# Padding SBUF pools so that matmul operands share an offset modulo 512, with a rewritten routing stage, in a hybrid diffusion block with 16 experts

## The chip, the cores and the metric

The kernel runs on one core of a Trainium2 chip. The metric is the device time of one execution in microseconds. Three runs of the kernel before gave 2228.50, 2229.75 and 2232.72 us.

## What is computed

One layer over 1024 tokens of width 1024, with 256 context tokens ahead of it: a conditioned RMSNorm, an input projection, a Hyena long convolution beside a gated linear recurrence, an output projection with a gated residual, then a mixture of 16 SwiGLU experts in which each expert picks its 128 best tokens, and a last RMSNorm. The change touches the output projection's second half, the routing and the experts. Of the reference, that is:

```python
x = x + g1 * mix                                # mix: concatenated mixer outputs @ w_out[l]
h2 = modulate(rmsnorm(x, norm2_g[l]), sh2, sc2)  # h * (1 + scale) + shift
x = x + g2 * ec_moe(h2, router_w[l], exp_w1[l], exp_w3[l], exp_w2[l])

def ec_moe(h, router_w, w1, w3, w2):
    aff = jax.nn.softmax(jnp.einsum('bnd,de->bne', h, router_w).astype(jnp.float32), axis=-1)
    gates, idx = lax.top_k(jnp.swapaxes(aff, 1, 2), cap)
    xg = jax.vmap(lambda hb, ib: hb[ib])(h, idx)
    a = jnp.einsum('becd,edf->becf', xg, w1)
    b = jnp.einsum('becd,edf->becf', xg, w3)
    y = jnp.einsum('becf,efd->becd', jax.nn.silu(a) * b, w2)
    y = y * gates[..., None].astype(y.dtype)
    return jax.vmap(lambda yb, ib: jnp.zeros((N, D), yb.dtype).at[ib.reshape(-1)].add(yb.reshape(-1, D)))(y, idx)
```

Here cap is 128, D is 1024 and the experts' inner width is 2048. All inputs are float32.

## The kernel before

**Split products.** A float32 product is made of three matmuls of type fp32r. Each operand is split into a high part and what is left of it, and `mm3` (lines 63 to 66) issues high by high (L64), high by low (L65) and low by high (L66) into one accumulating PSUM tile. The first operand of `mm3` is the stationary one, 128x128; the second moves, 128x512 in all the calls that matter here. In the profile's names, `pa<-ehi,hcT` is a matmul with the moving operand `ehi` and the stationary operand `hcT`.

**Output projection, second half.** For token tiles t = 0 to 7, `finish_h` (L999) projects the Hyena half of the mixer output and adds it into the residual tile `oxt`. The moving operand is `wo`. The stationary operand is `hcT` (the same buffers under the name mxA) for t = 0 to 3, and `mx` for t = 4 to 7. Beside it the tile runs through `normed` (a Square over 1024 columns on ACT, eleven small DVE operations for the inverse root in `rsqrt`, and a multiplication into `oh`), `flip` (eight PE transposes and eight scaled ACT copies of 128 columns, L1026), `route` (eight matmuls with the router's weights), `affinity` (softmax) and `rows8`, which transposes the result into the row tile R (L1054). The loop at L1056 runs 11 times, and a tile's routing lags its projection by three rounds.

**Search.** When R is complete, ten rounds on DVE (L1096 to L1113) find each expert's threshold: a count over R (L1097), a comparison, a small update of `base` (L1106), one PE matmul (L1108), and the new threshold (L1109). Meanwhile ACT casts the first three weight pieces to their high parts, and POOL subtracts to get their low parts (L1189). After the search the positions are counted on PE (L1129 to L1134), DVE builds a one-hot tile (L1150), PE makes indices from it (L1154), and POOL gathers the first expert's 128 rows (L1159).

**Experts.** The weights come as 384 pieces of 1 MiB, 24 to an expert, through a ring of 13 `raw` buffers filled by SP's queue (`fetch`, L993). Piece by piece ACT casts raw to `ehi` (L1185) and DVE subtracts to get `elo` (L1191), in a ring of three (NHI = 3). PE takes a piece by 12 matmuls of `mm3`, so an expert is 288 split matmuls and all sixteen are 4608. Two thirds have `hcT`, the gathered rows transposed, as stationary operand; one third has `hh`, the gated inner activations. `take` (L1213) lets the piece two ahead be split when PE's code for the present piece is written; there is no planner behind it. After each expert, POOL adds its rows into the output in DRAM (L1274).

**Addresses.** The tiles lie in SBUF pools one behind the other, so an added tile moves all that follows in its pool and in the pools behind. In the built program the offsets within a partition modulo 512 bytes are: hcT 96, mx 0, wo 0, ehi and elo 448, hh 288. Both operands of the input projection (hT, whi) are at 0.

## Time and profile before

| | us |
|---|---|
| median of three runs | 2229.75 |
| the profiled execution | 2229.96 |
| its span, first to last instruction | 2228.2 |
| output projection, second half (PE) | 931 to 984 |
| rest of the routing, search, first gather | 984 to 1046.5 |
| experts, first to last split matmul | 1046.5 to 2201.7 |
| sums and last norm | 2201.7 to 2228.2 |

The profiled execution spent 1.8 us outside its span. Times in the trace count from the first instruction. PE, DVE, ACT and POOL each run their own queue in order; a row of the timeline is a group of like instructions on one engine, and what stands in square brackets is the idle time before it and what ended that. Matmuls overlap, so a matmul's duration is longer than the distance between two starts; the distance is what counts.

### The profile page before, as it was taken

How to read it: one execution, taken by the hardware profiler on the slowest of the kernel's cores; microseconds unless marked ns; L12 is line 12 of the kernel's file. 1: busy time of each engine (PE TensorE's matmuls, PEld its weight loads, DVE VectorE, ACT ScalarE, POOL GpSimd, SP SyncE). 2: the span in 40 equal slices, each digit the busy share in tenths (PEclk: the TensorE clock that was granted, in tenths of full speed). 3: DMA queues.
4: the chain of work that ended last, by engine and by line, in shares of the span. 5: the costliest groups of instructions: out<-in, count | busy, mean ns of one | idle time of the engine just before them, and what ended most of it. 6: DMA issues, size and time to landing. Idle time of an engine off the chain costs nothing.

```text
span 2228.2 us, 30347 instructions
## 1 busy us (share of the span) xinstructions
PE 2073.0 (93%) x11727; PEld 1621.2 (73%) x11727; DVE 1741.0 (78%) x2033; ACT 1256.0 (56%) x1492; POOL 198.3 (9%) x234
## 2 busy tenths in 40 slices
PE   7996999899999998983999999999999999999997
PEld 2443877788788876762888887777777777777775
DVE  6688366647878886557888888888888888988887
ACT  3566235334432211261777777677777777777775
POOL 1121100100000001123000000000000000000000
PEclk9999999899999999995999999999999999999999
DMA  7875412221152447474999999999999999999992
GB/s 250 269 261 162 142 44 81 82 77 43 49 161 81 128 139 262 127 261 177 365 373 365 369 381 354 362 353 365 363 360 359 355 369 364 356 354 374 356 361 101
DMA packets 248124, 565.94 MB, mean 254 GB/s; under 512 B 15545, under 2 KB 26380, under 8 KB 247981
## 3 DMA queue, kind: packets, MB, share of 16 engines
q1 hardware_dynamic: 209620, 477.88, 59.9%
q0 software_dynamic: 28784, 76.46, 11.3%
q10 hardware_dynamic: 9576, 9.67, 1.3%
q8 instruction: 92, 1.51, 0.3%
q14 instruction: 52, 0.42, 0.1%
HBM read 522.59 MB, written 41.50 MB: 253 GB/s over the span
## 4 chain that ended last, share of the span: by engine, by line
PE 75%; DVE 10%; issue 6%; DMA 5%; ACT 4%; POOL 1%; DVEq 0%; ACTq 0%; SPq 0%; POOLq 0%
PE pa L65 15%; PE pa L66 14%; PE pa L64 14%; PE pb L65 5%; PE pb L66 5%; PE pb L64 5%; DVE elo L1191 2%; PE pt L861 2%; PE pb L842 2%; PE pf L543 2%; PE pt L1278 1%; ACT sa L1175 1%; DVE arena L724 1%; DVE arena L722 1%; DMA oraw<-in_w_out 1%
## 5 line engine op out<-in xcount | busy, mean ns | idle before, releaser
L1191 DVE TENSOR_TENSOR elo<-raw,ehi 128x2048 fp32r<-128x2048 f32 x381 | 863.8, 2288 | 107.8 <-ACT ehi L1185 106.6
L1185 ACT CAST ehi<-raw 128x2048 fp32r<-128x2048 f32 x384 | 732.9, 1914 | 175.1 <-PE pa L66 133.4
L65 PE MATMUL pa<-elo,hcT 128*128 128x512 f32 x1024 | 408.6, 399 | 17.0 <-DVE elo L1191 16.9
L64 PE MATMUL pa<-ehi,hcT 128*128 128x512 f32 x1024 | 409.5, 401 | 1.4 <-ACT hcT L1176 1.4
L66 PE MATMUL pa<-ehi,hcT 128*128 128x512 f32 x1024 | 404.2, 395 | 0.0
L65 PEld LDWEIGHTS pa<-elo,hcT 128*128 128x128 f32 x1024 | 192.8, 188 | 73.9 <-DVE elo L1191 32.3
L64 PEld LDWEIGHTS pa<-ehi,hcT 128*128 128x128 f32 x1024 | 192.7, 188 | 45.5 <-ACT hcT L1176 1.8
L66 PEld LDWEIGHTS pa<-ehi,hcT 128*128 128x128 f32 x1024 | 192.6, 188 | 45.4
L65 PE MATMUL pb<-elo,hh 128*128 128x512 f32 x512 | 205.9, 402 | 0.3 <-DVE elo L1191 0.3
L66 PE MATMUL pb<-ehi,hh 128*128 128x512 f32 x512 | 203.1, 397 | 0.0
L64 PE MATMUL pb<-ehi,hh 128*128 128x512 f32 x512 | 191.2, 396 | 0.7 <-ACT hh L1281 0.7
L64 PE MATMUL pa<-hT,whi 128*128 128x512 f32 x448 | 178.0, 397 | 0.0
L66 PE MATMUL pa<-hT,wlo 128*128 128x512 f32 x448 | 177.7, 397 | 0.3 <-DVE wlo L577 0.3
L65 PE MATMUL pa<-hT,whi 128*128 128x512 f32 x448 | 175.9, 393 | 0.0
L1274 POOL DMA_INDIRECT xacc<-xg,idx x15 | 45.4, 3023 | 813.7 <-DVE xg L1269 813.7
L64 PEld LDWEIGHTS pb<-ehi,hh 128*128 128x128 f32 x512 | 96.4, 188 | 24.3 <-ACT hh L1281 0.9
L65 PEld LDWEIGHTS pb<-elo,hh 128*128 128x128 f32 x512 | 96.5, 188 | 22.3 <-DVE elo L1191 0.7
L66 PEld LDWEIGHTS pb<-ehi,hh 128*128 128x128 f32 x512 | 96.5, 188 | 22.1 <-issue 0.5
L66 PEld LDWEIGHTS pa<-hT,wlo 128*128 128x128 f32 x448 | 84.1, 188 | 18.7 <-DVE wlo L577 1.3
L65 PEld LDWEIGHTS pa<-hT,whi 128*128 128x128 f32 x448 | 84.2, 188 | 17.0 <-issue 0.2
L64 PEld LDWEIGHTS pa<-hT,whi 128*128 128x128 f32 x448 | 84.2, 188 | 16.8 <-issue 0.2
L543 PE MATMUL pf<-Yh,mt 128*128 128x256 f32 x256 | 74.3, 424 | 17.9 <-ACT he L549 6.5
(398 smaller groups left out, 3136.6 us busy)
## 6 DMA issues: line engine op xcount, KB each, us to landing
raw<-in_exp_w SPq DMA_DIRECT2D x371, 1024.0 KB, 8.3
aw<-in_ada_w SPq DMA_DIRECT2D x96, 256.0 KB, 4.8
wraw<-in_w_in SPq DMA_DIRECT2D x64, 256.0 KB, 3.2
raw<-in_exp_w POOLq DMA_DIRECT2D x13, 1024.0 KB, 9.4
mt<-in_fwm POOLq DMA_DIRECT2D x64, 128.0 KB, 3.7
Hd<-he ACTq DMA_DIRECT2D x32, 256.0 KB, 2.9
wod<-arena POOLq DMA_DIRECT2D x32, 256.0 KB, 3.4
arena<-in_fwm SPq DMA_DIRECT2D x32, 256.0 KB, 6.1
```

The costliest lines, as they stand in the source:

```text
L64: PE.matmul(ps, lhs[0], rhs[0], start=first, stop=False)
L65: PE.matmul(ps, lhs[0], rhs[1], start=False, stop=False)
L66: PE.matmul(ps, lhs[1], rhs[0], start=False, stop=last)
L543: PE.matmul(pt[:, :HC], mt[:, i, :], Y[:, 2 * n + i, :], start=(i == 0), stop=(i == 1))
L722: V.tensor_tensor(kv, kv, view(F2, h, [[2 * h, nb], [LT - h, 2], [0, h]]), ALU.mult)
L724: V.tensor_tensor(qv, qv, view(F2, LT + h, [[2 * h, nq], [-(LT + h), 2], [0, h]]), ALU.mult)
L842: PE.matmul(px[:, j, :], fm[:, j, i, :], Y[:, 2 * n + i, :], start=(i == 0), stop=(i == 1))
L861: PE.matmul(pz[:, j, :], im[:, i, j, :], pp[:, i, :], start=(i == 0), stop=(i == 1))
L1175: S.activation(hf[:, c, :], pt[:, c * P:(c + 1) * P], AF.Identity, scale=gs2[:, k:k + 1], bias=mod2[:, k, 0:1])
L1185: S.copy(hi, raw)
L1191: V.tensor_tensor(lo, raw, f32(hi[:]), ALU.subtract)
L1274: G.indirect_dma_start(xacc[:], bass.IndirectOffsetOnAxis(ap=idx[:, 0:1], axis=0), xg[:, 0:D], None, compute_op=ALU.add)
```

## The change

Four things are done.

- Three unused tiles are allocated: 40 floats in the pool `late`, 112 in `op`, 40 in `ep`. After it every operand of the output projection's and the experts' split products is at 96 modulo 512. Five of the thirteen `raw` buffers (pool `eb`) and all `ehi` and `elo` move by 160 bytes; the other eight `raw` buffers stay.
- The routing stage works on the rows of `oxt` before their normalisation: the router's weights are scaled once (`router`), PE transposes `oxt`, two ACT copies of 512 columns take the place of the eight scaled ones, and the inverse root is applied to the 16 logits. The Square is made in two halves, the inverse root has one operation more, the loop runs 10 times with a shorter lag, and the multiplication into `oh2` moves into `rows8`.
- Two DVE operations of the search that read two SBUF tiles (L1106, L1113) become `tensor_scalar` with the second tile as a per-partition scalar.
- Nine 128x128 matmuls whose result nobody reads (`idle`) stand on PE after the two gathers are written.

```diff
--- before.py
+++ after.py
@@ -102,6 +102,7 @@
     ones = cst.tile([P, P], F32, name="ones")
     V.memset(ones, 1.0)
     masks = cst.tile([P, 5, 32], U32, name="masks")
+    pad = lambda pool, n: pool.tile([P, n], F32, name="pad")
 
     Hd = dram.tile([2, 2, 8, P, 2, HC], F32, name="Hd")
     yTd = dram.tile([2, 4, P, L], F32R, name="yTd")
@@ -889,12 +890,14 @@
     nc.gpsimd.dma_start(iot, T["iota"])
     tok = late.tile([P, 8, 2], BF16, name="tok")
     nc.gpsimd.dma_start(tok, T["tok"])
+    pad(late, 40)
     rmat = late.tile([P, 3, P], BF16, name="rmat")
     nc.gpsimd.dma_start(rmat, T["rmat"])
     jcol = late.tile([P, 10], F32, name="jcol")
     nc.scalar.dma_start(jcol, T["jcol"])
     octx = ctx.enter_context(ExitStack())
     op = octx.enter_context(tc.tile_pool(name="op", bufs=1))
+    pad(op, 112)
     rw = op.tile([P, 8, 32], F32, name="rw")
     nc.scalar.dma_start(rw, T["router_w"])
     sele = op.tile([P, NE], F32, name="sele")
@@ -957,7 +960,8 @@
 
         t = pool.tile([P, 4], F32, name=name, bufs=2)
         v, y, w = t[:, 0:1], t[:, 1:2], t[:, 2:3]
-        V.tensor_scalar(v, ssq, 1.0 / n, EPS, ALU.mult, ALU.add)
+        V.tensor_scalar(v, ssq[0], 1.0 / n, EPS, ALU.mult, ALU.add)
+        V.scalar_tensor_tensor(v, ssq[1], 1.0 / n, v, ALU.mult, ALU.add)
         V.tensor_scalar(y.bitcast(I32), v.bitcast(I32), -0.5, 1597463007.0, ALU.mult, ALU.add)
         for _ in range(3):
             V.scalar_tensor_tensor(w, v, -0.5, y, ALU.mult, ALU.mult)
@@ -996,40 +1000,54 @@
     tp = tctx.enter_context(tc.tile_pool(name="tp", bufs=1, side="right"))
     R = tp.tile([P, L], F32, name="R")
 
+
+    rwg = tp.tile([P, 8, 32], F32, name="rwg")
+    rws = tp.tile([P, 8, NE], F32, name="rws")
+    lb = tp.tile([P, NE], F32, name="lb")
+
+    def router():
+        V.tensor_tensor(rwg, rw, gs2[:].unsqueeze(2).broadcast_to([P, 8, 32]), ALU.mult)
+        V.tensor_tensor(rws, rw[:, :, 0:NE], mod2[:, 0:8, 0:1].broadcast_to([P, 8, NE]), ALU.mult)
+        pr = bank("pb", 2)
+        for k in range(8):
+            PE.matmul(pr[:, 0:NE], ones, rws[:, k, :], start=(k == 0), stop=(k == 7))
+        S.copy(lb, pr[:, 0:NE])
+
+    def after(ins):
+        return tc.issue_after(ins.ins if hasattr(ins, "ins") else ins)
+
+    tl = [{} for _ in range(8)]
+
     def finish_h(t, h):
         xh = xts[t][:, h * 512:(h + 1) * 512]
         V.scalar_tensor_tensor(xh, project(t, h, wo, my), yr[:, t:t + 1], xh, ALU.mult, ALU.add)
-
-    def after(ins):
-        return tc.issue_after(ins.ins if hasattr(ins, "ins") else ins)
-
-    tl = [{} for _ in range(8)]
-
-    def normed(t):
+        if h == 0:
+            tl[t]["h2"] = tp.tile([P, D + NE], F32, name="oh2", bufs=4)
+            tl[t]["st"] = tp.tile([P, 8], F32, name="ost", bufs=4)
+        S.activation(tl[t]["h2"][:, h * 512:(h + 1) * 512], xh, AF.Square, accum_out=tl[t]["st"][:, h:h + 1])
+
+    def stored(t):
         st_ = nc.gpsimd.dma_start(xacc[t * P:(t + 1) * P, :], xts[t])
         with after(st_):
             fetch(t, G)
-        h2 = tl[t]["h2"] = tp.tile([P, D + NE], F32, name="oh2", bufs=4)
-        st = tl[t]["st"] = tp.tile([P, 8], F32, name="ost", bufs=4)
-        S.activation(h2[:, 0:D], xts[t], AF.Square, accum_out=st[:, 0:1])
-        V.tensor_scalar(h2[:, 0:D], xts[t], rsqrt(tp, st[:, 0:1], D, "ors"), None, ALU.mult)
-
-    def flip(t):
-        h2 = tl[t]["h2"]
-        hTt = tl[t]["hT"] = tp.tile([P, 8, P], F32, name="h2T", bufs=1)
-        for b in range(2):
-            pt = bank("pt", 2)
-            for c in range(4):
-                PE.transpose(pt[:, c * P:(c + 1) * P], h2[:, (4 * b + c) * P:(4 * b + c + 1) * P], ident)
-            for c in range(4):
-                k = 4 * b + c
-                S.activation(hTt[:, k, :], pt[:, c * P:(c + 1) * P], AF.Identity, scale=gs2[:, k:k + 1], bias=mod2[:, k, 0:1])
+
+    def flip(t, b):
+        if b == 0:
+            tl[t]["hT"] = tp.tile([P, 8, P], F32, name="h2T", bufs=1)
+        pt = bank("pt", 2)
+        for c in range(4):
+            PE.transpose(pt[:, c * P:(c + 1) * P], xts[t][:, (4 * b + c) * P:(4 * b + c + 1) * P], ident)
+        S.copy(tl[t]["hT"][:, 4 * b:4 * b + 4, :], pt.rearrange("p (c t) -> p c t", t=P))
+
+    def scaled(t):
+        st = tl[t]["st"]
+        tl[t]["rs"] = rsqrt(tp, (st[:, 0:1], st[:, 1:2]), D, "ors")
 
     def route(t):
         pr = bank("pb", 2)
         for k in range(8):
             j = k % 4
-            PE.matmul(pr[32 * j:32 * j + 32, 0:P], rw[:, k, :], tl[t]["hT"][:, k, :], start=(k < 4), stop=(k >= 4))
+            PE.matmul(pr[32 * j:32 * j + 32, 0:P], rwg[:, k, :], tl[t]["hT"][:, k, :], start=(k < 4), stop=(k >= 4))
         lg = tl[t]["lg"] = tp.tile([P, P], F32, name="lg", bufs=2)
         S.copy(lg, pr[:, 0:P])
 
@@ -1037,36 +1055,44 @@
         h2, st = tl[t]["h2"], tl[t]["st"]
         pl = bank("pb", 2)
         PE.matmul(pl[:, 0:NE], tl[t]["lg"], sele, start=True, stop=True)
-        V.tensor_reduce(st[:, 3:4], pl[:, 0:NE], mybir.AxisListType.X, ALU.max, negate=True)
         ex = tp.tile([P, NE], F32, name="oex", bufs=2)
-        S.activation(ex, pl[:, 0:NE], AF.Exp, bias=st[:, 3:4], accum_out=st[:, 4:5])
+        V.scalar_tensor_tensor(ex, pl[:, 0:NE], tl[t]["rs"], lb, ALU.mult, ALU.add)
+        V.tensor_reduce(st[:, 3:4], ex, mybir.AxisListType.X, ALU.max, negate=True)
+        S.activation(ex, ex, AF.Exp, bias=st[:, 3:4], accum_out=st[:, 4:5])
         V.reciprocal(st[:, 5:6], st[:, 4:5])
-        V.tensor_scalar(aff[:, t, :], ex, st[:, 5:6], None, ALU.mult)
-        V.tensor_copy(h2[:, D:D + NE], aff[:, t, :])
-        tl[t]["stored"] = nc.gpsimd.dma_start(h2d[t * P:(t + 1) * P, :], h2)
 
         a8 = tl[t]["a8"] = tp.tile([P, NE, 8], F32, name="a8", bufs=2)
-        V.tensor_copy(a8, aff[:, t, :].unsqueeze(2).broadcast_to([P, NE, 8]))
+        V.tensor_scalar(a8, ex[:].unsqueeze(2).broadcast_to([P, NE, 8]), st[:, 5:6], None, ALU.mult)
 
     def rows8(t):
+        h2, st = tl[t]["h2"], tl[t]["st"]
         pa = bank("pb", 2)
         PE.transpose(pa[:, 0:P], tl[t]["a8"].rearrange("p e j -> p (e j)"), ident)
         tl[t]["row"] = S.copy(R[:, t * P:(t + 1) * P], pa[:, 0:P])
-
-    for t in range(11):
+        V.tensor_copy(aff[:, t, :], tl[t]["a8"][:, :, 0])
+        V.tensor_copy(h2[:, D:D + NE], aff[:, t, :])
+        V.tensor_scalar(h2[:, 0:D], xts[t], tl[t]["rs"], None, ALU.mult)
+        tl[t]["stored"] = nc.gpsimd.dma_start(h2d[t * P:(t + 1) * P, :], h2)
+
+    for t in range(10):
         if t < 8:
             finish_h(t, 0)
-        if 0 <= t - 2 < 8:
-            flip(t - 2)
-        if 0 <= t - 3:
-            affinity(t - 3)
+        if t == 0:
+            router()
+        if 1 <= t < 9:
+            scaled(t - 1)
+            flip(t - 1, 1)
+        if t >= 2:
+            affinity(t - 2)
         if t < 8:
             finish_h(t, 1)
-            normed(t)
-        if 0 <= t - 2 < 8:
-            route(t - 2)
-        if 0 <= t - 3:
-            rows8(t - 3)
+            stored(t)
+        if 1 <= t < 9:
+            route(t - 1)
+        if t < 8:
+            flip(t, 0)
+        if t >= 2:
+            rows8(t - 2)
     if "x1" in dbg:
         nc.sync.dma_start(dbg["x1"], xacc)
         nc.sync.dma_start(dbg["h2"], h2d)
@@ -1103,14 +1129,14 @@
         if r % 5 == 4:
             V.tensor_scalar(base[:, 1:2], base[:, 0:1], -float(sum(1 << (sh + 3 * q) for q in range(5))), None, ALU.add)
         else:
-            V.tensor_tensor(base[:, 1:2], jcol[:, r + 1:r + 2], base[:, 0:1], ALU.add)
+            V.tensor_scalar(base[:, 1:2], jcol[:, r + 1:r + 2], base[:, 0:1], None, ALU.add)
         pk = bank("pb", 2)
         PE.matmul(pk[:, 0:1], blk8, ind, start=True, stop=True)
         V.tensor_scalar(thr if r < 5 else low, pk[:, 0:1], float(1 << sh), base[:, 1:2], ALU.mult, ALU.add)
         if r == 4:
             V.tensor_scalar(bit, thr, 1 << 15, None, ALU.bitwise_and)
             V.tensor_copy(base[:, 0:1], bit)
-            V.tensor_tensor(low, jcol[:, 5:6], base[:, 0:1], ALU.add)
+            V.tensor_scalar(low, jcol[:, 5:6], base[:, 0:1], None, ALU.add)
 
 
     tw = tp.tile([P, P], F32, name="tw")
@@ -1198,6 +1224,7 @@
     nc.scalar.dma_start(fg, brow(T["final_g"], 0, D))
     ohT = hcT[0][:, :, 0:P]
     idf = ep.tile([P, 1], F32, name="idf")
+    pad(ep, 40)
     sums = {}
 
     def start_sum(t):
@@ -1223,6 +1250,10 @@
         fetch(n + NA + NB)
     g = {0: gather(0)}
     g[1] = gather(1)
+
+    idle = bank("pb", 2)
+    for _ in range(9):
+        PE.matmul(idle[:, 0:P], ident, ident, start=True, stop=True)
     xTs = {0: transposed(0, g[0][1])}
     py = None
     hs_ = {}
```

On ACT, the end of the routing stage and the first casts of weight pieces. `h2T` is the transposed tile, `lg` the logits, `oex` the exponentials, R the row tile, `oh` the place of the squares. Before:

```order
L1014 ACTIVATE oh_8292,ost<-oxt 128x1024
L1054 COPY R<-pb 128x128
L1026 ACTIVATE h2T<-pt,mod_78,gs_79 128x128 x8
L1042 ACTIVATE oex,ost<-pb,ost 128x16
L1034 COPY lg<-pb 128x128
L1026 ACTIVATE h2T<-pt,mod_78,gs_79 128x128 x3
L1054 COPY R<-pb 128x128
L1026 ACTIVATE h2T<-pt,mod_78,gs_79 128x128 x5
L1042 ACTIVATE oex,ost<-pb,ost 128x16
L1034 COPY lg<-pb 128x128
```

And after:

```order
L1027 ACTIVATE oh_8281,ost<-oxt 128x512
L1061 ACTIVATE oex,ost<-oex,ost 128x16
L1052 COPY lg<-pb 128x128
L1027 ACTIVATE oh_8281,ost<-oxt 128x512
L1040 COPY h2T<-pt 128x512
L1071 COPY R<-pb 128x128
L1040 COPY h2T<-pt 128x512
L1061 ACTIVATE oex,ost<-oex,ost 128x16
L1052 COPY lg<-pb 128x128
L1071 COPY R<-pb 128x128
```

Behind the last tile's square stood sixteen scaled copies of two tiles; now two copies of 512 columns stand there.

On DVE, one round of the search. `thr` is the threshold, `ind` the comparison, `pb` the PE result. Before:

```order
L1101 TENSOR_SCALAR base<-pb,base 128x1
L1097 TENSOR_SCALAR oh_8439,cnt<-R,thr 128x1024
L1106 TENSOR_TENSOR base<-jcol,base 128x1
L1098 TENSOR_SCALAR ind<-cnt 128x1
L1109 TENSOR_SCALAR thr<-pb,base 128x1
```

And after:

```order
L1127 TENSOR_SCALAR base<-pb,base 128x1
L1123 TENSOR_SCALAR oh_8432,cnt<-R,thr 128x1024
L1132 TENSOR_SCALAR base<-jcol,base 128x1
L1124 TENSOR_SCALAR ind<-cnt 128x1
L1135 TENSOR_SCALAR thr<-pb,base 128x1
```

Nothing moved; the third instruction has another form.

On PE, between the counting of positions (`rmat`) and the first expert's indices (`tok`, `oh`). Before:

```order
L1134 LDWEIGHTS rmat
L1134 MATMUL pb<-eq,rmat 128x32
L1134 LDWEIGHTS rmat
L1134 MATMUL pb<-eq,rmat 128x16
L1154 LDWEIGHTS oh
L1154 MATMUL pt<-tok,oh 128x1
```

And after:

```order
L1160 MATMUL pb<-eq,rmat 128x32
L1160 LDWEIGHTS rmat
L1160 MATMUL pb<-eq,rmat 128x16
L1256 MATMUL pb<-ident 128x128 x9
L1180 LDWEIGHTS oh
L1180 MATMUL pt<-tok,oh 128x1
```

The nine idle matmuls, written behind both gathers, stand on PE ahead of the first gather's index matmuls. In the expert stage PE, ACT, DVE and SP keep their order.

## Rows read from the trace of the kernel before

**Rows 1.** Windows: stretch, length, PE, PEld, DVE, ACT, POOL busy, PEclk, DMA share, GB/s.

```profile
998.00:1030.00 32.00, 1.51 (x9) 0.96 (x10) 29.48 (x56) 5.22 (x3) 17.09 (x8) 0.50 0.74 279
...
1150.00:1200.00 50.00, 50.00 (x223) 40.21 (x222) 43.49 (x27) 38.57 (x32) 0.86 (x1) 1.00 1.02 379
...
1046.50:2201.60 1155.10, 1137.20 (x5212) 906.14 (x5213) 995.19 (x609) 846.48 (x663) 70.43 (x29) 1.00 0.98 352
```

**Rows 2.** Timeline, PE, output projection: start, length, line, out<-moving,stationary, tiling, shape.

```profile
937.13 0.40 PE L64 MATMUL pa<-wo,hcT 128*128 128x512 f32 x1
...
942.53 0.39 PE L66 MATMUL pa<-wo,hcT 128*128 128x512 f32 x1
...
981.94 0.39 PE L64 MATMUL pa<-wo,mx 128*128 128x512 f32 x1
...
983.76 0.39 PE L66 MATMUL pa<-wo,mx 128*128 128x512 f32 x1
```

**Rows 3.** Summary of tiles wo and whi: count, duration ns min/median/max, first and last start.

```profile
L64 PE MATMUL pa<-wo,hcT x64: 391/398/796, 838.3 to 953.2; 128*128 128x512 f32 x64
L64 PE MATMUL pa<-wo,mx x64: 389/389/584, 870.5 to 983.3; 128*128 128x512 f32 x64
...
L64 PE MATMUL pa<-hT,whi x448: 387/389/792, 260.1 to 826.3; 128*128 128x512 f32 x150
```

**Rows 4.** Timeline, PE, inside the second expert's products.

```profile
1240.50 0.40 PE L64 MATMUL pa<-ehi,hcT 128*128 128x512 f32 x1
...
1247.97 0.40 PE L66 MATMUL pa<-ehi,hcT 128*128 128x512 f32 x1
```

**Rows 5.** Timeline of the search: DVE, second and third round and after it, POOL.

```profile
1001.02 0.15 DVE L1106 TENSOR_TENSOR base<-jcol,base 128x1 f32<-128x1 f32 x1
...
1003.04 13.39 DVE L1106 TENSOR_TENSOR base<-jcol,base 128x1 f32<-128x1 f32 x1
...
1034.98 0.29 DVE L1137 TENSOR_TENSOR posT<-pos,pos 128x128 bf16<-128x128 f32 x1
...
1002.99 13.41 POOL L1189 TENSOR_TENSOR elo<-raw,ehi 128x2048 fp32r<-128x2048 f32 x3
```

**Rows 6.** Timeline of ACT and DVE from the last projection to the last row of R.

```profile
985.03 1.06 ACT L1014 ACTIVATE oh<-oxt 128x1024 f32<-128x1024 f32 x1
...
986.22 2.92 ACT L1026 ACTIVATE h2T<-pt,mod,gs 128x128 f32<-128x128 f32 x8
...
997.50 0.27 ACT L1054 COPY R<-pb 128x128 f32<-128x128 f32 x1 [1.29 <-PE pb L1053]
...
988.35 0.75 DVE L1015 TENSOR_SCALAR oh<-oxt,ors 128x1024 f32<-128x1024 f32 x1
```

**Rows 7.** Timeline, POOL: the scatter that follows each expert, four of fifteen.

```profile
1203.73 1.60 POOL L1274 DMA_INDIRECT xacc<-xg,idx  x1 [52.87 <-DVE xg L1269]
...
1274.31 1.59 POOL L1274 DMA_INDIRECT xacc<-xg,idx  x1 [52.88 <-DVE xg L1269]
...
1415.83 3.38 POOL L1274 DMA_INDIRECT xacc<-xg,idx  x1 [53.73 <-DVE xg L1269]
...
1488.61 3.38 POOL L1274 DMA_INDIRECT xacc<-xg,idx  x1 [53.72 <-DVE xg L1269]
```

**Rows 8.** Waits: engine, line, what for: us in total, times, longest; last row SP's queue.

```profile
PEld pa L65 <- DVE elo L1191: 32.3, 42, 1.8
...
PE pa L65 <- DVE elo L1191: 16.9, 20, 1.4
...
SPq L993 <- DVE elo L1191: 975.2, 368, 38.9
```

**Rows 9.** Timeline, PE, from the counting to the first expert matmuls.

```profile
1036.63 0.56 PE L1154 MATMUL pt<-tok,oh 128*128 128x1 bf16 x16 [2.01 <-issue]
...
1047.54 0.63 PE L64 MATMUL pa<-ehi,hcT 128*128 128x512 f32 x1
1047.97 0.63 PE L65 MATMUL pa<-elo,hcT 128*128 128x512 f32 x1
```

## The prediction, made before the changed kernel ran

> **What bounds the kernel now.** I read the busy times by stage first, then the timeline of PE, then the waits. From 1046.5 to 2201.6 PE works on the experts and is busy for 1137.2 of 1155.1 us [rows 1]. More than half of the time is there, in 4608 split matmuls of one shape, so the question is what such a matmul costs.
>
> Its price is the distance between two starts, and it is not the same everywhere. In the output projection the 23 distances from 937.13 to 942.53 make 0.2348 us each where the operands are `wo` and `hcT`; the 8 from 981.94 to 983.76 make 0.2275 us where they are `wo` and `mx` [rows 2]. Line, loop, shape and moving operand are the same. What differs is the stationary tile: `hcT` lies 416 bytes modulo 512 away from `wo`, `mx` lies at the same offset. The median durations say the same over all such matmuls: 398 ns for `wo,hcT`, 389 for `wo,mx`, and again 389 for the 448 of `hT,whi`, which share their offset too [rows 3]. In the experts the 32 distances from 1240.50 to 1247.97 make 0.2334 us each [rows 4], and there the operands lie 352 or 160 apart. So the three sets of rows fit one reading: an unequal offset costs some 6 ns a matmul.
>
> From 984 to 1046.5 PE mostly waits, and the work goes through ACT and DVE. One item stands out there: a DVE addition of 128x1 that took 0.15 us a round earlier took 13.39 us, from 1003.04, while POOL made its three subtractions from 1002.99 for 13.41 us [rows 5].
>
> **The change part by part.** All is counted against the profiled execution, 2229.96 us, 1.8 of them outside the span; it lies 0.2 us above the median of the three runs, which I neglect.
>
> (a) *The search.* L1106 adds two SBUF tiles; it began 0.05 us after POOL and ended with it. In the new form it reads one tile and a scalar. If that keeps it clear of POOL, 13.39 − 0.15 = 13.2 us go from the path [rows 5]. What is late next? POOL's low parts are not wanted before the first expert matmul. But the next DVE instruction that reads two SBUF tiles is `posT`, at 1034.98 before. With 13.2 us of the search and the 4.5 us of (b) gone it comes at 1017.3; POOL's end at 1016.4 moves forward with (b) alone, to 1012. So there are 5 us of cover; without them `posT` would be caught as L1106 was. The new form isn't tested against POOL in this trace, nor is the count over R, which has one SBUF tile too: neither began while POOL was subtracting. Gain 13.2 us, with 0 as the other end.
>
> [...]
>
> (b) *The routing tail.* Tile 7's last projection matmul starts at 983.76 [rows 2], and its row of R is copied at 997.50 [rows 6]. From that path the change takes: half of the Square, 0.5 of 1.06; the multiplication into `oh`, 0.75, on which the transposes waited; and for each of the last two tiles 2.92 us of scaled copies, for which two copies of half the Square's width come in, about 2 × 0.6, so 1.7 twice [rows 6]. That makes 4.6; the inverse root gets one more small operation, 0.15 by the addition of that size [rows 5]. I take 4.5. The inverse root itself now runs beside the transposes instead of ahead of them; if it is late, some 2 us come back, and if the shorter lag hides more, 1.5 more go. Ends 2 and 6.
>
> (c) *Output projection.* 96 matmuls of each half pair `wo` with `hcT`. At 0.2348 − 0.2275 = 7 ns [rows 2] that is 1.4 us for both halves; the first half also waits for transfers, so 1 us, ends 0 and 1.4.
>
> (d) *The experts.* Per matmul 0.2334 − 0.2275 = 5.9 ns [rows 2, 4]; 4608 of them make 27 us if PE alone sets the pace. It doesn't quite. The second to fourth experts take 70.58 us each (1203.73 to 1274.31), later ones 72.78 (1415.83 to 1488.61) [rows 7]. The difference of 2.2 us is PE waiting for the low part of a weight piece, 32.3 + 16.9 = 49 us in 62 waits [rows 8]. The cast and the subtraction of a piece can start when PE frees a buffer of the ring of three, two pieces or 24 matmuls ahead. That chain keeps its length while the 24 matmuls become shorter by 24 × 5.9 ns = 0.14 us; over 62 waits that gives 9 us back if each wait stands alone, and nothing if those that stand close together share one chain. I take 5, so a gain of 22. The lower end is 12, if in the later experts more pieces come to wait; the upper is 30, if the experts' other pairs lie halfway to the 0.2348 of [rows 2].
>
> DMA is close behind. In the second expert 379 GB/s moved, and the whole stage had 352 on average [rows 1]. A cycle shorter by 1.5 us in 72 wants the same bytes 2% faster. But SP's queue waited 975 us in 368 waits for DVE to free a buffer [rows 8], so each transfer starts a whole ring ahead of its use. I count no cost here and keep the case as a rival.
>
> [...]
>
> (e) *Idle matmuls.* PE was granted half clock through the search [rows 1], and at the experts' start too: 0.43 us from 1047.54 to 1047.97 [rows 9] against 0.233. Seven matmuls stand so there, which costs 7 × 0.2 = 1.4 us, and the transposes ahead of them up to half as much again. Nine idle matmuls, which are a quarter as wide but of plain float32, I bound by the 128x512 ones: 3.9 us at half clock, 1.9 if they were half as dear. PE had stood still for 2.01 us before the first indices [rows 9] while DVE made the one-hot; the idle matmuls fit into that, or delay the gather by up to 1.9 us. Gain up to 2.1, loss up to 1.9; I take 0.
>
> Sum: 13.2 + 4.5 + 1 + 22 + 0 = 40.7 us, so 2229.96 − 40.7 = **2189 us**. With the ends of (b) to (e), and (a) as it is, 2177 to 2205.
>
> **The rivals.** *A, offsets do nothing.* The `hcT` matmuls may be dear for another reason, such as other traffic at their place. For it speaks that no row shows `hcT` at an equal offset; against it, that 64 matmuls of either kind, spread over both halves of one loop, differ by 9 ns in the median [rows 3]. Then (c) and (d) vanish: 2229.96 − 17.7 = 2212 us. [...]
>
> *B, the search still waits.* The count over R or the new update is shut out by POOL as L1106 was, for the same 13.4 us, an instruction earlier or later. Then (a) vanishes: 2202 us. [...] For it: no one-source operation begins during a POOL subtraction [rows 5].
>
> *C, the weights set the pace.* If transfers can hold little more than the stage's 352 GB/s [rows 1], the experts gain between nothing and 10 of the 22 us: 2201 to 2211 us. For it: the DMA share is at 0.98 to 1.02. Against it: 379 GB/s over 50 us, and buffers, not transfers, that SP waits for.
>
> *D, slower.* The pads move five of the thirteen `raw` buffers by 160 bytes, and so the place where each row of their transfers lands. If that slows these transfers, the ring runs empty and PE waits for weights. The other terms give 18.7 us, so D decides from an expert stage longer by 19 us, which is an average below 352 × 1155 / 1174 = 346 GB/s. At 340 the stage takes 1196 us, and the kernel 2229.96 − 18.7 + 41 = 2252 us. For it: other landing places have not been tried. Against it: the waits show no transfer that is late now.
>
> **How the numbers follow.** Forecast 0.60, A 0.11, B 0.11, C 0.11, D 0.03. The remaining 0.04 is for two at once: A or C with B leaves (b) and little else, 2215 to 2226 us. 0.2%, 4.5 us, is about what a measurement of this kernel can tell from no change; only D and the end of the double cases are not faster by that. So faster 0.94, same 0.03, slower 0.03. The range goes from 2177, the low end of the sum, to 2212, which takes in B, C and A; D, the double cases and a part of the forecast's own tails stay outside.
>
> **What would show it.** Right: starts of the experts' matmuls 0.227 to 0.229 us apart and medians of 389 ns; `wo,hcT` like `wo,mx`; every update of `base` in the search at about 0.15 us, also during POOL's subtractions; the first expert matmul at about 1028; scatters 69 us apart for the second to fourth expert and about 71.4 later, with somewhat longer waits for `elo`. Wrong: matmuls still 0.233 us apart (A); a DVE row of 10 us or more beside POOL (B); PE or ACT waiting for `raw`, and a DMA rate that stays below 360 GB/s (C, or D if also slower).

## The result

The changed kernel took 2194.53 us (median of four runs, 2189.97 to 2197.76), the kernel before 2231.23 us beside it. The ratio is 0.9832, with a 95% interval of 0.9804 to 0.986. So the change gained some 37 us (31 to 44 by the interval); the forecast was 41, at 2189 us, in a range of 2177 to 2212. The profiled execution of the changed kernel took 2197.11 us.

One statement ahead of the prediction was off: both operands of the input projection lie at 96 modulo 512, not at 0. Their difference is 0, and only that was used.

The page of the changed kernel, its parts 1 and 4:

```profile
PE 2049.8 (93%) x11761; PEld 1621.8 (74%) x11761; DVE 1731.7 (79%) x2051; ACT 1243.2 (57%) x1461; POOL 198.4 (9%) x234
...
PE 72%; DVE 11%; issue 6%; DMA 6%; ACT 4%; POOL 1%; DVEq 0%; ACTq 0%; SPq 0%; POOLq 0%
```

PE is still the engine that sets the end.

The same inside of an expert as in [rows 4], now of the changed kernel (timeline, PE). Below it are the summary of the tile `ehi` before, and the summaries of `ehi` and `wo` of the changed kernel (count, duration in ns min/median/max, first and last start):

```profile
1225.50 0.39 PE L64 MATMUL pa<-ehi,hcT 128*128 128x512 f32 x1
...
1231.85 0.39 PE L65 MATMUL pa<-elo,hcT 128*128 128x512 f32 x1
```

```profile
L64 PE MATMUL pa<-ehi,hcT x1024: 388/399/794, 1046.5 to 2186.1; 128*128 128x512 f32 x171
...
L64 PE MATMUL pb<-ehi,hh x512: 391/397/500, 1071.0 to 2201.0; 128*128 128x512 f32 x171
```

```profile
L64 PE MATMUL pa<-ehi,hcT x1024: 387/389/796, 1035.2 to 2153.4; 128*128 128x512 f32 x171
L64 PE MATMUL pb<-ehi,hh x512: 387/389/497, 1059.4 to 2168.2; 128*128 128x512 f32 x171
L64 PE MATMUL pa<-wo,hcT x64: 389/393/796, 844.2 to 960.5; 128*128 128x512 f32 x64
L64 PE MATMUL pa<-wo,mx x64: 387/392/585, 876.7 to 990.5; 128*128 128x512 f32 x64
```

The 28 distances from 1225.50 to 1231.85 make 0.2268 us each, where 0.2334 stood in [rows 4]. The medians of the experts have come from 399 and 397 to 389 ns. `wo,hcT` has come down from 398 [rows 3] to 393, which is what `wo,mx` has now (392; it was at 389). By the median distance between two starts, `wo,hcT` went from 235 to 227 ns, and `wo,mx` was and is at 227.

The search of the changed kernel (timelines of DVE, POOL and PE); L1132 is the update of `base`, L1163 is `posT`:

```profile
1005.58 0.21 DVE L1132 TENSOR_SCALAR base<-jcol,base 128x1 f32<-128x1 f32 x1
...
1016.16 0.21 DVE L1132 TENSOR_SCALAR base<-jcol,base 128x1 f32<-128x1 f32 x1
...
1022.42 0.29 DVE L1163 TENSOR_TENSOR posT<-pos,pos 128x128 bf16<-128x128 f32 x1
```

```profile
1004.32 13.46 POOL L1215 TENSOR_TENSOR elo<-raw,ehi 128x2048 fp32r<-128x2048 f32 x3
```

POOL subtracts from 1004.32 to 1017.78, and five updates and the counts between them run through that time at the length that they have elsewhere (0.21 and 1.27 us); [rows 5] had one update of 13.39 us there. `posT`, which reads two SBUF tiles, comes 4.6 us after POOL's end.

The scatters, as in [rows 7] (timeline, POOL), and the waits, as in [rows 8]:

```profile
1189.07 1.60 POOL L1305 DMA_INDIRECT xacc<-xg,idx  x1 [51.56 <-DVE xg L1300]
...
1257.88 1.59 POOL L1305 DMA_INDIRECT xacc<-xg,idx  x1 [51.54 <-DVE xg L1300]
...
1396.19 3.38 POOL L1305 DMA_INDIRECT xacc<-xg,idx  x1 [52.74 <-DVE xg L1300]
...
1467.80 3.38 POOL L1305 DMA_INDIRECT xacc<-xg,idx  x1 [52.78 <-DVE xg L1300]
```

```profile
PEld pa L65 <- DVE elo L1217: 34.7, 42, 1.9
...
PE pa L65 <- DVE elo L1217: 18.5, 20, 1.5
...
ACT ehi L1211 <- DMA raw<-in_exp_w: 7.0, 8, 1.3
```

An early expert takes 68.81 us instead of 70.58, a later one 71.61 instead of 72.78. The waits for `elo` have grown from 49.2 to 53.2 us, in 62 places both times. The first line is idle time of the weight loads (PEld), which overlap the matmuls (busy for 74% of the span beside PE's 93%); PE itself waited 16.9 us before [rows 8] and 18.5 now. ACT now waits 7.0 us for transfers of `raw`; PE doesn't.

Where the time went, in stretches that are read from the timelines: A from the first to the last `wo` matmul of the projection's second half; B from there to the last row of R; C from there to the first gather; D from there to the first expert matmul; E the experts, from the first to the last split matmul; F the rest. All in us, of the profiled execution of each kernel; the names of the experiments are those of the next section.

| kernel | A | B | C | D | E | F |
|---|---|---|---|---|---|---|
| before | 57.8 | 13.7 | 40.2 | 8.8 | 1154.9 | 26.8 |
| changed | 61.0 | 7.2 | 28.4 | 8.7 | 1133.5 | 26.7 |
| e1, pads only | 57.9 | 13.7 | 40.2 | 8.7 | 1134.8 | 26.7 |
| e2, search only | 58.0 | 13.8 | 27.0 | 8.4 | 1155.3 | 26.8 |
| e3, routing only | 61.5 | 7.2 | 40.9 | 8.6 | 1155.5 | 26.8 |
| e4, changed, no idle matmuls | 60.9 | 7.1 | 27.0 | 8.5 | 1134.2 | 26.7 |
| e7, idle matmuls later | 61.1 | 7.1 | 27.0 | 8.2 | 1131.9 | 26.7 |
| e8, ring of four | 61.2 | 7.1 | 29.1 | 9.4 | 1126.0 | 26.6 |
| e9, e7 and e8 | 61.4 | 7.2 | 29.1 | 8.6 | 1123.2 | 26.6 |

Before and changed differ by 36.8 us in these stretches, as the medians do (36.7). The spans of the two profiled executions differ by only 32.9, because the second half's first matmul came at 926.0 before and at 930.0 in the changed kernel. That place scatters from 922.7 to 930.0 over all the profiles of this study, although the instructions ahead of it, but for the pads, are the same; so the stretches tell the parts apart better than the spans. It is also why one sign of the prediction was missed: the first expert matmul came at 1035.2, not at about 1028. Of these 7 us, 4.0 are the later start of the projection's second half, and the others lie in A to D.

In that half PE of these kernels stands still once, some 6 us behind its first matmul, for a transfer of `wo`: 0.60 us before, 1.05 in e1, 0.80 in e2, 0.84 in e3, 0.54 in the changed kernel. Without this wait A is 57.2 us before and in e2, 56.9 in e1, 60.7 in e3 and 60.4 in the changed kernel.

### The profile page after: what moved, and what is told of

It is laid out like the page before. It is cut to its first block, busy times and chain, and to the rows that moved or that the text cites. A ratio compares the mean times of both kernels' runs of the same rounds, so it can differ in the third digit from the quotient of the medians.

```text
span 2195.3 us, 30395 instructions
## 1 busy us (share of the span) xinstructions
PE 2049.8 (93%) x11761; PEld 1621.8 (74%) x11761; DVE 1731.7 (79%) x2051; ACT 1243.2 (57%) x1461; POOL 198.4 (9%) x234
## 3 DMA queue, kind: packets, MB, share of 16 engines
q1 hardware_dynamic: 209620, 477.88, 60.4%
## 4 chain that ended last, share of the span: by engine, by line
PE 72%; DVE 11%; issue 6%; DMA 6%; ACT 4%; POOL 1%; DVEq 0%; ACTq 0%; SPq 0%; POOLq 0%
PE pa L65 14%; PE pa L66 14%; PE pa L64 13%; PE pb L66 5%; PE pb L65 5%; PE pb L64 5%; DVE elo L1217 4%; PE pt L862 2%; PE pb L843 2%; PE pf L544 2%; ACT sa L1201 1%; DMA oraw<-in_w_out 1%; PE pt L1309 1%; DVE arena L725 1%; DVE arena L723 1%
## 5 line engine op out<-in xcount | busy, mean ns | idle before, releaser
L65 PE MATMUL pa<-elo,hcT 128*128 128x512 f32 x1024 | 405.5, 396 | 19.5 <-DVE elo L1217 18.5
L64 PE MATMUL pa<-ehi,hcT 128*128 128x512 f32 x1024 | 403.1, 395 | 1.4 <-ACT hcT L1202 1.4
L66 PE MATMUL pa<-ehi,hcT 128*128 128x512 f32 x1024 | 399.8, 391 | 0.0
L66 PE MATMUL pb<-ehi,hh 128*128 128x512 f32 x512 | 200.5, 392 | 0.0
L64 PE MATMUL pb<-ehi,hh 128*128 128x512 f32 x512 | 187.9, 390 | 0.7 <-ACT hh L1312 0.7
L65 PEld LDWEIGHTS pb<-elo,hh 128*128 128x128 f32 x512 | 96.2, 188 | 20.1 <-DVE elo L1217 0.8
L65 PEld LDWEIGHTS pa<-hT,whi 128*128 128x128 f32 x448 | 84.2, 188 | 16.9 <-issue 0.2
```

The source lines that it names most:

```text
L64: PE.matmul(ps, lhs[0], rhs[0], start=first, stop=False)
L65: PE.matmul(ps, lhs[0], rhs[1], start=False, stop=False)
L66: PE.matmul(ps, lhs[1], rhs[0], start=False, stop=last)
```

## The experiments

**One part alone.** Three kernels have one part of the change each. Pads only (the three `pad` lines of the diff, nothing else):

> The kernel before with the three pads and nothing else. If the offsets are what made the matmuls dear, the experts take 1133.5 us from first to last split matmul as in the changed kernel (1154.9 before), the distances of wo,hcT, ehi,hcT and ehi,hh fall to a median of 227 ns, and the time is 21 to 23 us under the kernel before. If the matmuls became cheaper by something else that the change did (other code ahead of them, another clock), the distances stay at 231 to 237 ns and the time stays within 2 us of before.

Measured: 2208.84 us, ratio 0.9896 [0.9875, 0.9917], so 22.6 us less. E is 1134.8, and the summary of tile `ehi` in this kernel has

```profile
L64 PE MATMUL pa<-ehi,hcT x1024: 387/389/792, 1049.2 to 2168.7; 128*128 128x512 f32 x171
L64 PE MATMUL pb<-ehi,hh x512: 387/389/497, 1074.6 to 2183.5; 128*128 128x512 f32 x171
```

No instruction differs from the kernel before, so the experts' gain comes from where the tiles lie.

Search only:

```diff
-            V.tensor_tensor(base[:, 1:2], jcol[:, r + 1:r + 2], base[:, 0:1], ALU.add)
+            V.tensor_scalar(base[:, 1:2], jcol[:, r + 1:r + 2], base[:, 0:1], None, ALU.add)
...
-            V.tensor_tensor(low, jcol[:, 5:6], base[:, 0:1], ALU.add)
+            V.tensor_scalar(low, jcol[:, 5:6], base[:, 0:1], None, ALU.add)
```

> The kernel before with the two single-source operations of the search and nothing else. If two SBUF sources are what POOL's subtraction shut out, the search loses its 13.4 us row and the kernel 13.2 us; the matmuls stay at 234 ns. If it was only the moment at which the update met POOL, that is if the earlier routing tail of the changed kernel moved the meeting away, the update is caught here as before and the time stays.

Measured: 2216.05 us, ratio 0.9932 [0.991, 0.9955], 15.4 us less; C falls by 13.1. In this kernel POOL and the search meet as they did before: an update begins 0.05 us behind POOL's first subtraction, as in [rows 5], and it and the next one are short (timelines, POOL and DVE):

```profile
1004.01 13.43 POOL L1189 TENSOR_TENSOR elo<-raw,ehi 128x2048 fp32r<-128x2048 f32 x3
```

```profile
1004.06 0.21 DVE L1106 TENSOR_SCALAR base<-jcol,base 128x1 f32<-128x1 f32 x1
...
1006.04 0.21 DVE L1106 TENSOR_SCALAR base<-jcol,base 128x1 f32<-128x1 f32 x1
```

So it is the form with two SBUF sources that was held (13.39 us [rows 5], against 0.21 here), and not the moment.

Routing only: the changed kernel without the four `pad` lines and the idle matmuls, and with the two `tensor_tensor` lines of the search as before.

> The kernel before with the rewritten routing stage and nothing else (no pads, two-source updates, no idle matmuls). The stretch from the last wo matmul to the last row of R falls from 13.7 to 7.2 us, so the time by 6.5 us, if the tail is worth what the two traces show. If the tail's gain came partly from the equal offsets in the projection, it is smaller. One update of the search is caught by POOL for some 13.4 us, as before.

Measured: 2229.29 us, ratio 0.9986 [0.9974, 0.9998], 2.2 us less. B falls by 6.5 as expected, but A grows by 3.7 (3.5 without its wait for `wo`), which the expectation had not, and C by 0.7, because one update was caught a little longer (timelines, DVE and POOL):

```profile
999.68 14.12 DVE L1129 TENSOR_TENSOR base<-jcol,base 128x1 f32<-128x1 f32 x1
```

```profile
1000.36 4.51 POOL L1212 TENSOR_TENSOR elo<-raw,ehi 128x2048 fp32r<-128x2048 f32 x1
```

Here the update stands 0.68 us ahead of POOL's first subtraction and still ends with the third. POOL was then on the last of five issues of `raw` transfers (999.60 to 1000.35). The update before it took 0.15 us beside another of these issues, so what held this one during the first 0.68 us is not shown.

**Why the projection became longer.** One kernel, without idle matmuls, leaves out seven of the eight products that make the bias of the logits, so that its routing is another:

```diff
-        for k in range(8):
-            PE.matmul(pr[:, 0:NE], ones, rws[:, k, :], start=(k == 0), stop=(k == 7))
+        PE.matmul(pr[:, 0:NE], ones, rws[:, 0, :], start=True, stop=True)
```

> The changed kernel without idle matmuls and with one of the eight products that make the bias of the logits; the other seven are left out, so the routing is another. If the router's matmuls lie on PE's path in the projection, its stretch with hcT (31.0 us with all eight) falls by about 7/8 of 1.85 us, to 29.4. If they fit into gaps, it stays at 31.0, and the 3.2 us by which the rewritten routing lengthens this stretch are all the transposes and route matmuls of the tile that now runs earlier.

Measured in one execution, of 2192.29 us: the stretch with `hcT` takes 30.1 us, against 31.0 in e4 (the changed kernel without idle matmuls, below) and 27.7 before. In this execution the stretch waited 1.20 us for `wo`, against 0.58 in e4, so the router's matmuls account for 0.9 us as read and for some 1.6 without that difference. The timeline of the changed kernel shows them on PE between products:

```profile
938.00 1.85 PE L1013 MATMUL pb<-rws,ones 128*128 128x16 f32 x16
```

The rest is work of the tile that now runs one round earlier. No run takes it out by itself, but the PE timelines of both kernels show it in this stretch: 24 transposes and 32 passes of route matmuls where 16 and 16 stood. Counted to the next start on PE, the transposes take 2.4 us instead of 1.7 and the route matmuls 1.15 instead of 0.57. With the router's 1.7 that makes 3.0 of the 3.3 us.

**The idle matmuls.** The changed kernel without them:

> The changed kernel without its nine idle matmuls. By the trace of the changed kernel they delay the first index matmuls by 1.6 us and the clock is back at half by the first gathered rows, so without them the stretch from the counting to the first expert matmul is shorter by 1.6 us and the first seven expert matmuls stand 0.43 us apart as with them. If they do warm the clock for the experts, the stretch is shorter but the first expert matmuls are slower by up to 1.4 us, and nothing is gained.

Measured: 2194.21 us, against 2194.53 with them. C is 27.0 instead of 28.4, and C and D together 1.6 us shorter. E is 0.8 longer. In the changed kernel (windows: busy times, then PEclk, DMA share, GB/s; and timeline, PE):

```profile
1021.00:1026.00 5.00, 5.00 (x48) 4.93 (x45) 1.85 (x4) 0.00 (x0) 0.00 (x0) 0.60 0.92 342
...
1031.00:1034.00 3.00, 1.97 (x8) 1.57 (x8) 0.14 (x1) 0.99 (x3) 0.00 (x0) 0.50 0.65 184
```

```profile
1021.90 3.75 PE L1256 MATMUL pb<-ident 128*128 128x128 f32 x18
1025.49 0.54 PE L1180 MATMUL pt<-tok,oh 128*128 128x1 bf16 x16
```

The idle matmuls run almost wholly at half clock (0.50 up to 1025), 3.75 us, and push the first index matmuls from 2.0 to 3.6 us behind the counting. The clock does rise, to 0.98 for the last 1.0 us of the first window. Then PE has nearly nothing to do while the rows are gathered (0.58 us from 1026 to 1031), and when their transposes begin, the granted clock is at 0.50 again.

The 0.8 us in E can't be put down to the idle matmuls. At the start of the first expert, 8 matmuls of the changed kernel stand more than 0.3 us behind the one ahead, at half clock (0.50 from 1036 to 1038), and 12 of e4; but without idle matmuls it was 7 before, and 14, 8 and 9 in e1, e2 and e3. Each costs 0.2 us (0.427 against 0.227), so such a difference comes and goes with the execution.

Twelve idle matmuls placed later (each appears as two passes in the trace), tied to the first expert's index so that they can't run before it:

```diff
-    for _ in range(9):
-        PE.matmul(idle[:, 0:P], ident, ident, start=True, stop=True)
+    for _ in range(12):
+        PE.matmul(idle[:, 0:P], ident, g[0][0].bitcast(F32).broadcast_to([P, P]), start=True, stop=True)
```

> The changed kernel with twelve idle matmuls that read the first expert's index, so that they stand behind the first index matmuls and run while the gathered rows are on their way, and not ahead of the gather. If PE's activity in that wait brings the full clock for what follows, the first gathered rows' transposes take about 1.1 us instead of 1.97, the first expert matmuls stand 0.23 us apart instead of 0.43, and the gather isn't delayed: 1.6 us for the delay, 0.8 and 1.4 for the clock, together 3.8 us less than the changed kernel from the counting to the eighth expert matmul. If the clock falls back in whatever pause is left, only the 1.6 us are gained.

Measured: 2190.18 us, 0.9824 [0.9791, 0.9858], which the runs can't tell from the changed kernel; the stretches can. The timeline of PE:

```profile
1021.41 2.93 PE L1256 MATMUL pb<-idx,ident 128*128 128x128 f32 x12 [0.25 <-DVE idx L1182]
1024.13 0.61 PE L1180 MATMUL pt<-tok,oh 128*128 128x1 bf16 x16
1024.60 2.33 PE L1256 MATMUL pb<-idx,ident 128*128 128x128 f32 x12
1026.91 1.09 PE L1195 MATMUL pt<-ident,xg 128*128 128x128 f32 x8
1029.82 0.50 PE L64 MATMUL pa<-ehi,hcT 128*128 128x512 f32 x1 [1.81 <-ACT hcT L1202]
1030.15 0.40 PE L65 MATMUL pa<-elo,hcT 128*128 128x512 f32 x1
```

PE works up to the moment when the rows are there, the eight transposes take 1.09 us instead of 1.97, and the experts start at full clock (PEclk 0.95 from 1026 to 1028, 1.00 from 1028 to 1030): only the first distance is over 0.3 us (0.33). C, D and E together are 3.4 us shorter than in the changed kernel, where 3.8 were expected up to the eighth expert matmul.

**Which offsets are cheap.** Two kernels differ from the changed one in the sizes of the pads alone (24, 176 and 104 floats; 32, 176 and 72):

> The changed kernel with other pad sizes, so that the operands lie apart modulo 512 by 448 bytes (ehi, elo against hcT), 256 (ehi, elo against hh) and 192 (wo against hcT); wo and mx stay equal. If only equality modulo 512 is cheap, all three pairs go back to medians of 231 to 237 ns and the experts take about 1155 us. If the cheap set is wider, for instance equality modulo 256, the pair at 256 stays at 227 ns. If any offset does that is a multiple of 64, all stay at 227.

> As the run before, with 480 bytes (ehi, elo against hcT), 384 (ehi, elo against hh) and 224 (wo against hcT). If equality modulo 512 is what counts, all three are at 231 to 237 ns. If the price grows with the distance, 480, which is 32 bytes from equal, is nearer to 227 than the others; if the pairs at 384 stay cheap, equality modulo 128 is enough.

Measured, each in one execution, 2205.13 and 2211.07 us. Summaries of the tiles in the first of the two; `ehi` and `hcT` are 448 apart, `ehi` and `hh` 256, `wo` and `hcT` 192, `wo` and `mx` 0:

```profile
L64 PE MATMUL pa<-ehi,hcT x1024: 390/394/796, 1029.8 to 2161.4; 128*128 128x512 f32 x171
L64 PE MATMUL pb<-ehi,hh x512: 387/389/498, 1054.4 to 2176.1; 128*128 128x512 f32 x171
```

```profile
L64 PE MATMUL pa<-wo,hcT x64: 392/398/794, 840.9 to 955.4; 128*128 128x512 f32 x64
L64 PE MATMUL pa<-wo,mx x64: 387/389/585, 872.0 to 985.2; 128*128 128x512 f32 x64
```

And in the second, with `ehi` and `hcT` 480 apart, `ehi` and `hh` 384:

```profile
L64 PE MATMUL pa<-ehi,hcT x1024: 387/396/792, 1028.4 to 2166.6; 128*128 128x512 f32 x171
L64 PE MATMUL pb<-ehi,hh x512: 390/393/499, 1054.2 to 2181.4; 128*128 128x512 f32 x171
```

The pair at 256 is as cheap as the pairs at 0; 448, 192, 480 and 384 are dear, and so is `wo` with `hcT` at 224 in the second kernel (a median of 396 ns). Median distances between two starts, over all matmuls of a pair: 227 ns at 0 and 256, 232 to 235 at the others (and 232 to 235 before, at 352, 160 and 416). E is 1146.8 in the first, where two thirds of the experts' matmuls are dear, and 1153.5 in the second. So among the ten differences seen (0, 160, 192, 224, 256, 352, 384, 416, 448, 480) the two that are equal modulo 256 are cheap, a wider set than the change aims at, and being 32 bytes from equal doesn't help. The 256 rests on one pair of tiles, and differences of 32 to 128, 288 and 320 were not measured.

**What holds the later experts.** Four `ehi` and `elo` buffers instead of three, in the room of two `raw` buffers (eleven are left), with pieces split three ahead and without idle matmuls:

```diff
-    NA, NB, NHI = 8, 5, 3
+    NA, NB, NHI = 8, 3, 4
...
-            if n < NHI:
+            if n < 3:
...
-        if at > 0:
-            split(at + NHI - 1)
-            fetch(at + NHI - 1 + NA + NB)
+        for n in ([3, 4] if at == 1 else [at + NHI - 1] if at > 1 else []):
+            split(n)
+            fetch(n + NA + NB)
...
-    for n in range(NHI):
+    for n in range(3):
```

> The changed kernel without idle matmuls, with four ehi and elo buffers instead of three and three late raw buffers instead of five (same room), and with PE's code taking pieces three ahead. If the ring of three is what leaves PE waiting for elo in the later experts, these fall from 71.6 to about 68.9 us each and the time by some 30 us. If the weights' transfers set the pace there, the waits move from elo to raw, the rate stays near 370 GB/s and most of the gain is missing. If ACT and DVE are simply late in those places by their own order, the waits for elo stay as they are.

Measured: 2189.39 us, 0.9816 [0.9783, 0.9849]. E falls by 8.2 us from e4's to 1126.0, a later expert takes 70.67 instead of 71.6, an early one 68.84 as before. The waits:

```profile
PEld pa L65 <- DVE elo L1217: 26.3, 45, 1.0
...
PE pa L65 <- DVE elo L1217: 9.0, 21, 0.6
...
DVE elo L1217 <- DMA raw<-in_exp_w: 4.5, 6, 1.4
```

The waits for `elo` fall from 53.2 to 35.3 us in 66 places; PE's own among them, the second line, fall from 18.5 to 9.0, which is about what E gained. None of the three expectations holds alone: the ring accounts for about a third of what the later experts lose against the early ones, and waits for transfers are small. Of the other two thirds (70.67 against 68.84), 0.8 us of an expert are still PE's own waits for `elo`; what the rest is, no run shows. C grows by 2.1 us; e9 shows why.

The ring of four and the late idle matmuls together:

> The changed kernel with the ring of four of one earlier run and the idle matmuls behind the first index matmuls of another. If the two gains are independent, the experts take some 1124 us (1126.0 with the ring alone, 1131.9 with the late idle matmuls alone, 1134.2 with neither) and the stretch from the last row of R to the first expert matmul about 35 to 38 us; the time is 8 to 13 us under the changed kernel's 2194.5. If the fuller start only lets PE reach the waits for elo sooner, the experts stay at 1126 and the gain is the ring's alone.

Measured: 2185.53 us, 0.9805 [0.9789, 0.982], the lowest median of all. E is 1123.2, 2.7 us under e8's; late idle matmuls gave 2.3 with a ring of three (e7 against e4). So the two gains add up. The timeline of DVE ahead of the first gather:

```profile
1015.65 0.29 DVE L1163 TENSOR_TENSOR posT<-pos,pos 128x128 bf16<-128x128 f32 x1
1015.87 2.29 DVE L1217 TENSOR_TENSOR elo<-raw,ehi 128x2048 fp32r<-128x2048 f32 x1
1018.07 1.22 DVE L1176 TENSOR_TENSOR oh<-iot,posT 128x1024 bf16<-128x1024 bf16 x1
```

The fourth piece's subtraction stands ahead of the one-hot that the gather waits for, which is the 2.1 us.

## Why the prediction was right, step by step

*(a) The search*, 13.2 forecast: 13.1 in C (e2, and e4 against before). The cover that (a) named, 5 us between POOL's end and `posT`, was 4.6. Rival B falls: counts and updates with one SBUF source ran through the whole of POOL's subtractions, at 1.27 and 0.21 us each (e2). The old form cost 13.38 and 14.12 us in e1 and e3: an update that took 0.15 us a round earlier was held through three subtractions of 4.5 us each.

*(b) The routing tail*, 4.5 forecast: 3.0 by e3, which is 6.5 less in B and, without the wait for `wo`, 3.5 more in A (as read, A and B are 68.7 in e3, and 71.5 to 71.8 in the kernels with the old routing). This term was mis-sized twice. The tail gained more than I had worked out from the copies and the Square. But `router`, a part of the diff, had no term at all, and its sixteen passes take 1.85 us on PE; and a shorter lag moves PE work into the projection, where PE is the engine that is waited for. I had treated the lag as a gain only. That the sum stayed inside the ends of 2 and 6 is luck: the two errors, 2 us and 3.5, went opposite ways.

*(c) The projection*, 1 forecast: 0.3 in the second half, with the old routing (57.2 to 56.9, e1) as with the new (60.7 to 60.4), both without the wait for `wo`. In e1 that wait was longer by 0.45 us, so as read the pads changed nothing in A (57.9 against 57.8). The first half takes 84.7 us in the changed kernel and 84.3 in e3, which has no pads, and 82.3 to 88.0 over all the kernels, so its share can't be read.

*(d) The experts*, 22 forecast: 21.4 from before to changed, 20.1 by e1. Put on the same number of half-clock matmuls at the start (7 before, 8 changed, 14 in e1), it is 21.6 and 21.5. An early expert gained 1.77 us, which is 288 matmuls by 6.1 ns, and a later one 1.2. So the 5 us that I gave back to the ring were about right in size, but not in the way I got them: of the 49 us in 62 waits that I took for PE's, 32.3 are the weight loads'. PE's own waits for `elo` grew only from 16.9 to 18.5 us, 20 waits both times, and what else kept the later experts from the full 1.77 is not shown.

Rival A falls with e1: pads alone change the price, from medians of 399 and 397 ns to 389. e5 adds that within one kernel and one execution the pair at 256 is cheap (389) and the pair at 448 dear (394), which other traffic can't explain. What makes the difference by place, 227 against 233 ns from one start to the next, is not shown by any run.

*Rival C* is not what happened. The changed kernel moved 389 GB/s in its best window of 50 us, 10 more than the best before, and 358 over the stage against 352 [rows 1]. The 7.0 us that ACT waited for transfers, against 1.8 in two waits before, show that it isn't far (e4, with the same experts, had 3.8), but PE never waited for a weight transfer there. *Rival D* falls with e1 as well: five raw buffers lie elsewhere, and nothing became slower.

*(e) The idle matmuls*, 0 forecast with ends of −2.1 and +1.9: they cost 1.6 us ahead of the gather, and nothing that they give back is shown (e4). The upper bound by the 128x512 at half clock, 3.9 us, was close to the 3.75 measured, and I should have taken it: PE had been at half clock all through the search (0.50 [rows 1]). In the gain of up to 2.1, half as much again for the transposes, 0.7 us, was my estimate; with the clock up they took 0.88 less (1.97 to 1.09, e7).

Of the 40.7 us forecast, the stretches show 36.8. What is missing is 2.1 us in A and B, where (b) and (c) had 5.5; 1.3 in C and D, where (a) had 13.2 and (e) nothing; and 0.6 in E. The other 1.3 us between 2189 and the 2194.5 measured are the base: I counted from 2229.96, and the median beside the changed kernel was 2231.23.

## What to carry to other kernels

Before a matmul loop is called full, compare the distances of its starts with those of another loop of the same shape: here some 6 ns by 4608 matmuls were worth 21.4 us, where the rewritten routing gave 3.0, and they cost three unused tiles. A small operation that lasts far too long is looked up beside the other engines' operations of that moment, and another form of it is tried: here an addition of two SBUF tiles took 13.39 us beside POOL's subtractions, and 0.21 us with one tile and a scalar (e2). Idle matmuls are best placed so that they end where the real work begins: up to the transposes, they left a granted clock of 0.95 there (e7); placed ahead of something that is waited for, they were a delay of 1.6 us, and the clock was back at 0.50.

## What the runs showed of the hardware that I had not expected

- 128x512 fp32r matmuls stand a median of 227 ns apart when their operands' offsets within the partition differ by 0 or 256 bytes modulo 512, and 232 to 235 ns at 160, 192, 224, 352, 384, 416, 448 and 480. Even at 32 bytes from equal (480) they are dear, with a median duration of 396 ns (e6), and 256 is as good as 0, with 389 (e5).
- A DVE addition of 128x1 that reads two SBUF tiles was held through three POOL subtractions in a row, 13.38 us (e1) and more, and with one tile and a per-partition scalar it took 0.21 us at the same place (e2). In e3 it was held even though the trace starts it 0.68 us ahead of the first subtraction.
- The granted clock stood at 0.50 while idle matmuls ran from 1021.90 to 1025, and at 0.98 from 1025 to 1026. From 1026 to 1031 PE was busy for 0.58 us; the clock was at 1.00 up to 1028, at 0.50 from 1029, and still at 0.50 at the first transposes (changed kernel). With idle matmuls up to the transposes it was at 0.95 from 1026 to 1028 and at 1.00 from 1028 to 1030 (e7).
- The time from the start to the projection's second half scatters by 7 us (922.7 to 930.0) over profiles whose work there is the same.
